# Weight groups 5 to 10 loaded in four pieces of 32 partitions, each later piece held back to a later attention unit

## The chip, the cores and the metric

One Trainium2 chip, one of its cores. The program is launched once for the whole layer. The metric is the device time of one execution in microseconds (us), lower is better; where several runs are given, their median counts. The core has five engines with instruction queues of their own, which run in order: TensorE (PE, with its weight loads shown apart as PEld), VectorE (DVE), ScalarE (ACT), GpSimd (POOL) and SyncE (SP). SP's queue (SPq) issues nearly all of the DMAs here, the DMA transposes among them; POOL issues the loads of the weights.

## The reference

One layer over 1024 tokens of width 1024, in float32: an RMS norm, one input projection to 3328 columns, two groups of heads that read the same projected input, a SiLU gate on each, one output projection, the residual and a last RMS norm.

```python
h = _rmsnorm(x, norm_gain[l])
proj = h @ w_in[l]
q_a, k_a, v_a, g_a, q_b, k_b, v_b, g_b = jnp.split(proj, split_at, axis=-1)
q_a = _rmsnorm(q_a.reshape(b, s, A_HEADS, HEAD_DIM), q_norm_a[l])
k_a = _rmsnorm(k_a.reshape(b, s, A_KV_HEADS, HEAD_DIM), k_norm_a[l])
q_a = q_a * cos + _rotate_half_axial(q_a) * sin
k_a = k_a * cos + _rotate_half_axial(k_a) * sin
o_a = _gqa_blocked(q_a, k_a, v_a) * jax.nn.silu(g_a)
o_b = _neighbourhood_attn(q_b, k_b, v_b, na_rpb[l]) * jax.nn.silu(g_b)
x = x + jnp.concatenate([o_a, o_b], axis=-1) @ w_out[l]
return _rmsnorm(x, final_norm_gain)
```

Group A is full attention with 8 query heads and 2 key/value heads; group B is attention over a window of a 16 by 64 token grid. (Reshapes and the per-head details of group B are cut.)

## The kernel before

The columns of the input projection are cut into 13 groups of 256 (0 is k and v of group A, 1 and 2 its queries, 3 and 4 the queries of B, 5 and 6 its keys, 7 and 8 its values, 9 to 12 the gates), those of the output projection into four more (13 to 16). Every product is done with float32 numbers split into a high and a low half of 16 bits, so each group of weights goes through four steps:

- `load_w(g)`: 1 MB from memory into the tile `raw{g}`, 128 partitions by 8 KB. There are two such buffers (`wraw`, bufs=2), so the load of group g + 2 waits until group g has been split.
- `prep_a(g)`, L280: ACT squares `raw{g}` and sums it up.
- `prep_b(g)`, L292 to L294: PE, DVE and POOL turn the sum into a scale; the last step is a power on POOL (L294).
- `prep_c(g)` and `prep_d(g)`, L299 and L306: ACT writes the high half, DVE the low half, into `whl{g}`. From then on PE may use the group.

`Flow` strings the work together in slots. `step` runs, in this order, what is due at "pre", a first piece of work, what is due at "mid", a second one, what is due at "post", then some pieces of projection from a queue (`fill`), and a last one. `at(n, pos, fn)` puts `fn` n slots later at that position. When a group has been split, `sums_now` puts `load_w(g + 2)` two slots later at "pre".

Stage A is 64 units (head half, block of 128 queries, head), one for each slot. Unit i has `a_qk` as its first piece: four matmuls give the scores `s` (L591, L593), DVE finds the maximum (L600) and writes it into the small tile `nm`, ACT takes the exponential (L602) and the high half of it (L603). One slot later `a_lo` takes the low half on DVE (L608) and issues from SP a DMA transpose of both halves, 128 x 2048 x 2 bytes (L613, `ar<-ar` or `pt<-ar`). Four slots after `a_qk` (SKEW_A = 4) `a_pv` multiplies the transposed probabilities with the values (L622 to L624). Between these, PE works on projection groups 3 to 8 in small pieces of 6 matmuls (L368, tiles `pj`, `wt`, `kb`). Their results are brought into shape by ACT and DVE, and for the queries of B by one more transpose each (L504), for the keys of B by four plain DMAs (L537, tile `khh`).

PE runs in the order in which the program is written. Outside the opening, the order on ACT, DVE, POOL and SP is settled by a scheduler when the program is built. Weight groups 5 to 10 are loaded in stage A or right ahead of it; POOL has little else to do there, but at the load of group 5 it is still busy with the rotary step of group A's queries (`norm_rope`: L416, L424, L428).

A load can be gated: a one-column copy into the tile that is to be loaded (L157), from a tile that must exist first, makes the DMA behind it wait. Groups 2 and 3 use that.

Of the kernel before, what the change touches and what calls it, by code (L numbers as in the profile page):

```python
# [43 lines left out]
class Flow:  # L44
# [8 lines left out]
    def at(self, delay, pos, fn, *a):  # L53
        self.due.setdefault((self.slot + delay, pos), []).append((fn, a))
# [35 lines left out]
def kernel(ctx: ExitStack, tc: tile.TileContext, x: bass.AP, w: bass.AP, wo: bass.AP,  # L90
# [3 lines left out]
    act, dve, pool, pe, sp = nc.scalar, nc.vector, nc.gpsimd, nc.tensor, nc.sync  # L94
# [10 lines left out]
    at = fl.at  # L105
# [12 lines left out]
    def carve(store, off, shape, dt):  # L118

        n = 4 if dt == F32 else 2  # L120
        t = store[:, off // 4:off // 4 + int(np.prod(shape)) * n // 4]
        t = t if n == 4 else t.bitcast(dt)
        if len(shape) == 1:
            return t
        names = "abcdef"[:len(shape)]
        return t.rearrange(f"p ({' '.join(names)}) -> p {' '.join(names)}", **dict(zip(names, shape)))
# [21 lines left out]
    def tn(name, n=1, tag="t"):  # L148
        return tiny.tile([P, n], F32, tag=tag, name=name)


    raw, wp, late, x2 = {}, {}, {}, {}

    def load_w(g):
        raw[g] = wraw.tile([P, KC, GC], F32, tag="raw", name=f"raw{g}")
        if g in gate:
            pool.tensor_copy(raw[g][:, 0, :1], xr[gate[g]][:, 1:])  # L157
        pool.dma_start(raw[g], w[g] if g < 13 else wo[g - 13])

    xts, gate = [], {}  # L160
    ones = area(0, [P], F32)[:1]
# [35 lines left out]
    def col(i, n=1):  # L197
        return sm[:, i:i + n]
# [141 lines left out]
    def sums_now():  # L340

        while pend:
            g = pend.pop(0)
            prep_b(g)
            at(1, "pre", prep_c, g)
            at(1, "post", prep_d, g)
            if g + 2 < 17:
                at(2, "pre", load_w, g + 2)
# [238 lines left out]
    def a_qk(i, hh, u, h):  # L587
        s = ps_s.tile([P, 1024], F32, tag="s", name=f"s{hh}_{u}_{h}")
        q = qTa[hh][:, u, h]
        for c in range(2):  # L590
            pe.matmul(s[:, c * 512:(c + 1) * 512], q, kTa[:, 4 * c:4 * c + 4, hh], start=True, stop=False)  # L591
        for c in range(2):
            pe.matmul(s[:, c * 512:(c + 1) * 512], q, klo1[:, 4 * c:4 * c + 4] if hh else kTa[:, 4 * c:4 * c + 4, 2],  # L593
                      start=False, stop=True)
        if h == 0:
            sums[hh, u] = tn(f"sum{hh}_{u}", 4, "sum")
        nm = tn(f"nm{hh}_{u}_{h}")
        o = 4096 * (i % RING)
        hl, p32 = carve(ar, o, [2, 1024], F16), carve(ar, o + 2048, [1024], F32)
        dve.tensor_tensor_reduce(out=hl[:, 1].bitcast(BF16), in0=s, in1=col(SHA).to_broadcast([P, 1024]), scale=col(NSA),  # L600
                                 scalar=3e38, op0=OP.add, op1=OP.min, accum_out=nm)
        act.activation(p32, s, AF.Exp, bias=nm, scale=col(SCA), accum_out=sums[hh, u][:, h:h + 1])  # L602
        at(0, "post", lambda: act.activation(hl[:, 0], p32, AF.Copy))  # L603
        hls[hh, u, h] = (hl, p32)
# [266 lines left out]
    x_rs(7)  # L871
    x_y(7)
    load_w(2)
    gate[3] = 5
    x_lo(7, dve)
    load_w(3)

    for p in range(11):
# [33 lines left out]
    n_head = sum(n for n, _ in FILL_A)  # L912
    mid = (6 * 32 - sum(n * r for n, r in FILL_A) - FILL_A_END * SKEW_A) / (64 - n_head) + 0.02
    run_units(ua, SKEW_A, a_qk, a_lo, a_pv, rates(FILL_A + [(64 - n_head, mid)], FILL_A_END))
    fl.fill(1000)

# [127 lines left out]
```

## Time and profile before

| | us |
|---|---|
| median of 3 runs | 599.39 |
| the 3 runs | 599.29, 599.39, 605.95 |
| profiled execution, its time | 600.28 |
| profiled execution, its span (first to last instruction) | 598.5 |
| PE busy | 530.8 (89% of the span) |
| DVE busy | 440.9 (74%) |
| ACT busy | 391.0 (65%) |
| POOL busy | 121.8 (20%) |
| mean granted TensorE clock | 0.974 |

Times in the profile are counted from the first instruction of the span. A row of the timeline reads: start, duration, engine, line, operation, the tile written and the tiles read, and in square brackets the idle time of the engine just before it and what ended it. In the chain of waits each row is a start, a duration and what the time was spent on; a row "DMA ar<-ar" there is the time from a transpose's issue to its landing. Stage A runs from about 105 us to about 350 us.

### The profile page before, as it was taken

The numbers are of one execution on the slowest core, as the hardware profiler recorded it, in microseconds if no ns is written. First come the engines' busy times: TensorE is split into PE (matmuls) and PEld (weight loads), VectorE is DVE, ScalarE is ACT, GpSimd is POOL, SyncE is SP. The second block draws the span as 40 slices with busy tenths as digits, with TensorE's granted clock in tenths as the row PEclk, the third lists the DMA queues.
The fourth block names the chain that finished last, engine by engine and source line by source line (L and its number), as shares of the span: only waits on it lengthen the run. The fifth ranks groups of instructions, "written<-read, shape, count | busy, mean of one in ns | idle before, by whom it ended". The sixth has DMA issues, their size and how long they took to land.

```text
span 598.5 us, 13870 instructions
## 1 busy us (share of the span) xinstructions
PE 530.8 (89%) x5541; PEld 404.4 (68%) x5541; DVE 440.9 (74%) x986; ACT 391.0 (65%) x647; POOL 121.8 (20%) x150
## 2 busy tenths in 40 slices
PE   2587989979979989998989979999999789889894
PEld 1366878758856545556768857887877567668684
DVE  4689676987978968975988947585878767778332
ACT  5553445777768858875868826677779986774210
POOL 2395788510100000000100000010111221122100
PEclk9979989989999989999899999999999899999898
DMA  8989533799999999999899983467576996699422
GB/s 233 225 162 243 112 108 68 143 187 215 195 192 188 206 209 181 221 191 208 179 188 213 230 214 79 90 133 96 128 116 123 180 200 146 138 146 190 92 61 70
DMA packets 245972, 97.26 MB, mean 162 GB/s; under 512 B 236562, under 2 KB 237202, under 8 KB 243987
## 3 DMA queue, kind: packets, MB, share of 16 engines
q1 hardware_dynamic: 242306, 75.66, 70.8%
q0 software_dynamic: 3312, 19.92, 11.7%
q8 instruction: 43, 0.70, 0.5%
q10 hardware_dynamic: 288, 0.79, 0.5%
q14 instruction: 23, 0.18, 0.1%
HBM read 31.33 MB, written 4.19 MB: 59 GB/s over the span
## 4 chain that ended last, share of the span: by engine, by line
PE 48%; DMA 18%; DVE 14%; issue 8%; ACT 5%; POOL 4%; SPq 1%; DVEq 0%; POOLq 0%; ACTq 0%
PE pj L368 15%; DMA ar<-ar 10%; PE wt L368 8%; PE kb L368 5%; PE po L368 4%; PE s L591 3%; PE s L593 3%; PE pv L622 2%; PE pv L624 2%; PE pv L623 2%; DVE whl L306 2%; DMA ar<-mhl 2%; POOL nt L416 1%; PE sb L675 1%; DMA x2b<-in_x_dram 1%
## 5 line engine op out<-in xcount | busy, mean ns | idle before, releaser
L368 PEld LDWEIGHTS <-hT 128*128 128x128 f16 x2112 | 205.8, 100 | 68.9 <-DMA hT<-xhl 14.7
L368 PE MATMUL pj<-whl,hT 128*128 128x256 f16 x1584 | 187.6, 274 | 3.9 <-DMA hT<-xhl 2.5
L602 ACT ACTIVATE ar<-s,nm,sm 128x1024 f32<-128x1024 f32 x64 | 76.9, 1202 | 43.6 <-DVE nm L600 35.8
L600 DVE CUSTOM_DVE_ANT_0 ar<-s,sm 128x1024 bf16<-128x1024 f32 x64 | 81.9, 1279 | 18.9 <-PE s L593 18.6
L368 PE MATMUL wt<-whl,hT 128*128 128x256 f16 x528 | 70.9, 294 | 13.8 <-ACT whl L299 7.1
L608 DVE TENSOR_TENSOR ar<-ar 128x1024 f16<-128x1024 f32 x64 | 77.9, 1218 | 5.4 <-ACT ar L603 5.4
L603 ACT ACTIVATE ar<-ar 128x1024 f16<-128x1024 f32 x64 | 67.5, 1056 | 6.5 <-DVE ar L608 5.3
L368 PE MATMUL po<-whl,mA 128*128 128x256 f16 x384 | 65.8, 277 | 0.0
L685 ACT ACTIVATE rq<-ar,mx,sm 128x384 f32<-128x384 f32 (+1 forms) x64 | 43.0, 672 | 30.8 <-DVE mx L684 30.6
L294 POOL TENSOR_TENSOR sm<-wss,mh 128x1 f32<-128x1 f32 x17 | 12.7, 749 | 240.4 <-DVE wss L293 160.6
L368 PEld LDWEIGHTS <-mA 128*128 128x128 f16 x512 | 48.8, 100 | 12.5 <-issue 5.3
L368 PE MATMUL po<-whl,ar 128*128 128x256 f16 x192 | 53.1, 277 | 0.0
L622 PE MATMUL pv<-va,ar 128*128 128x64 f16 x384 | 39.9, 195 | 12.0 <-DMA ar<-ar 12.0
L306 DVE SCALAR_TENSOR_TENSOR whl<-raw,sm,whl 128x1024 f16<-128x1024 f32 (+1 forms) x33 | 44.7, 1371 | 2.3 <-ACT whl L299 2.3
L622 PEld LDWEIGHTS <-ar 128*128 128x128 f16 x384 | 35.1, 99 | 16.6 <-DMA ar<-ar 14.3
L686 ACT ACTIVATE ar<-ar,mx,sm 128x384 f16<-128x384 f32 (+1 forms) x64 | 42.8, 673 | 1.0
L299 ACT ACTIVATE whl<-raw,sm 128x1024 f16<-128x1024 f32 x34 | 37.0, 1136 | 5.9 <-POOL sm L294 5.8
L624 PE MATMUL pv<-va,ar 128*128 128x64 f16 x384 | 39.9, 195 | 0.0
L623 PE MATMUL pv<-va,ar 128*128 128x64 f16 x384 | 39.8, 195 | 0.0
L591 PE MATMUL s<-kTa,rq 128*128 128x512 f16 x128 | 39.4, 391 | 0.3 <-ACT ar L602 0.3
L682 DVE CUSTOM_DVE_ANT_0 ar<-sb,bias 128x384 f32<-128x384 f32 x48 | 26.6, 554 | 17.2 <-PE sb L675 14.3
L691 DVE TENSOR_TENSOR ar<-rq,ar 128x384 f16<-128x384 f32 (+1 forms) x64 | 34.1, 533 | 4.4 <-ACT ar L686 4.4
(183 smaller groups left out, 1012.2 us busy)
## 6 DMA issues: line engine op xcount, KB each, us to landing
raw<-in_w_dram POOLq DMA_DIRECT2D x11, 1024.0 KB, 6.3
raw<-in_wo_dram POOLq DMA_DIRECT2D x4, 1024.0 KB, 6.1
ar<-in_x_dram SPq DMA_DIRECT2D x7, 512.0 KB, 6.4
khh<-ar SPq DMA_DIRECT2D x16, 128.0 KB, 4.1
x2b<-in_x_dram POOLq DMA_DIRECT2D x4, 512.0 KB, 6.4
x<-in_x_dram POOLq DMA_DIRECT2D x4, 512.0 KB, 6.3
out_dram<-x2b SPq DMA_DIRECT2D x8, 256.0 KB, 3.3
ar<-ar SPq DMA_TRANSPOSE x112, 4.5
```

What stands on the lines that cost most here:

```text
L306: dve.scalar_tensor_tensor(wp[g][1][:, s], raw[g][:, s], col(S_ + g), wp[g][0][:, s], op0=OP.mult, op1=OP.subtract)
L368: pe.matmul(*o[0], **o[1])
L591: pe.matmul(s[:, c * 512:(c + 1) * 512], q, kTa[:, 4 * c:4 * c + 4, hh], start=True, stop=False)
L600: dve.tensor_tensor_reduce(out=hl[:, 1].bitcast(BF16), in0=s, in1=col(SHA).to_broadcast([P, 1024]), scale=col(NSA), scalar=3e38, op0=OP.ad ...
L602: act.activation(p32, s, AF.Exp, bias=nm, scale=col(SCA), accum_out=sums[hh, u][:, h:h + 1])
L603: at(0, "post", lambda: act.activation(hl[:, 0], p32, AF.Copy))
L608: dve.tensor_tensor(hl[:, 1], p32, hl[:, 0], op=OP.subtract)
L622: pe.matmul(o, pt[:, kt], va[:, kt, hh, 0], start=kt == 0, stop=False)
L623: pe.matmul(o, pt[:, kt], va[:, kt, hh, 1], start=False, stop=False)
L624: pe.matmul(o, pt[:, 8 + kt], va[:, kt, hh, 0], start=False, stop=kt == 7)
L685: act.activation(p32, t, AF.Exp, bias=mx, scale=col(SCB + hh), accum_out=sums["b", u][:, h:h + 1])
L686: act.activation(hl[:, 0], t, AF.Exp, bias=mx, scale=col(SCB + hh))
```

## The change

Only `load_w` and one line of `a_qk` differ. For groups 5 to 10 the one load of 1 MB becomes four of 256 KB, each of 32 partitions by 8 KB. Piece 0 is issued where the whole load was. Pieces 1, 2 and 3 are put one, two and three slots later, at "post"; each has ahead of it on POOL a one-column copy of the newest `nm` into its own 32 partitions, so that it can't start before DVE has found the maximum of the unit of that slot. `late["nm"]` is where `a_qk` leaves that tile.

```diff
         if g in gate:
             pool.tensor_copy(raw[g][:, 0, :1], xr[gate[g]][:, 1:])
-        pool.dma_start(raw[g], w[g] if g < 13 else wo[g - 13])
+        src = w[g] if g < 13 else wo[g - 13]
+        if not 5 <= g < 11:
+            pool.dma_start(raw[g], src)
+            return
+
+        def piece(j):
+            r = slice(32 * j, 32 * j + 32)
+            if j:
+                pool.tensor_copy(raw[g][r, 0, :1], late["nm"][r])
+            pool.dma_start(raw[g][r], src[r])
+        piece(0)
+        for j in range(1, 4):
+            at(j, "post", piece, j)
...
-        nm = tn(f"nm{hh}_{u}_{h}")
+        nm = late["nm"] = tn(f"nm{hh}_{u}_{h}")
```

PE, DVE, ACT and SP have the same instructions in the same order as before. POOL has 36 rows more: 18 copies and 18 DMA issues. All lines behind the edit stand 12 lines lower in the changed kernel (L294 is L306 there, L416 is L428, L424 is L436, L428 is L440).

POOL at the load of group 5 (`raw_1066`), where stage A begins, before; `nt` and `tabs` belong to the rotary step, `sm` holds the scales of the weights:

```order
L158 DMA raw_1066<-in_w_dram 128x2048
L416 TENSOR_TENSOR nt_2_993<-nt_2_993,mh 128x8
L424 TENSOR_TENSOR ar<-ar,tabs 128x8x32 x2
L428 TENSOR_TENSOR ar<-ar 128x512
L416 TENSOR_TENSOR nt_3_1061<-nt_3_1061,mh 128x8
L424 TENSOR_TENSOR ar<-ar,tabs 128x8x32 x2
L428 TENSOR_TENSOR ar<-ar 128x512
L294 TENSOR_TENSOR sm<-wss_1198,mh 128x1
```

The same place of the changed kernel; `nm_0_1` is the maximum of unit 1, and so on:

```order
L167 DMA raw_1066<-in_w_dram 32x2048
L428 TENSOR_TENSOR nt_2_993<-nt_2_993,mh 128x8
L436 TENSOR_TENSOR ar<-ar,tabs 128x8x32 x2
L440 TENSOR_TENSOR ar<-ar 128x512
L428 TENSOR_TENSOR nt_3_1061<-nt_3_1061,mh 128x8
L166 COPY raw_1066<-nm_0_1_1122 32x1
L167 DMA raw_1066<-in_w_dram 32x2048
L436 TENSOR_TENSOR ar<-ar,tabs 128x8x32 x2
L166 COPY raw_1066<-nm_0_2_1163 32x1
L167 DMA raw_1066<-in_w_dram 32x2048
L440 TENSOR_TENSOR ar<-ar 128x512
L166 COPY raw_1066<-nm_0_3_1209 32x1
```

Pieces 1 and 2 of group 5 now stand ahead of the last two steps of the rotary work; the third stands behind it.

POOL at the load of group 7 (`raw_1848`), in the middle of stage A, before:

```order
L294 TENSOR_TENSOR sm<-wss_1616,mh 128x1
L158 DMA raw_1848<-in_w_dram 128x2048
L294 TENSOR_TENSOR sm<-wss_2278,mh 128x1
```

And of the changed kernel, where the tile is `raw_1860`; `nm_3_3` is unit 15, `nm_4_0` unit 16, `nm_4_1` unit 17:

```order
L306 TENSOR_TENSOR sm<-wss_1628,mh 128x1
L167 DMA raw_1860<-in_w_dram 32x2048
L166 COPY raw_1860<-nm_3_3_1927 32x1
L167 DMA raw_1860<-in_w_dram 32x2048
L166 COPY raw_1860<-nm_4_0_1977 32x1
L167 DMA raw_1860<-in_w_dram 32x2048
L166 COPY raw_1860<-nm_4_1_2039 32x1
L167 DMA raw_1860<-in_w_dram 32x2048
L306 TENSOR_TENSOR sm<-wss_2296,mh 128x1
```

The three later pieces follow their units with nothing else between; the loads of groups 6, 8, 9 and 10 look the same.

## The prediction

> **What bounds the kernel now.** I read the page first, for the busy shares, then PE's timeline in stage A for where PE stands idle, then the chain of waits for what ended each of these gaps, then POOL's timeline for the weight loads. The page's first lines:
>
> ```profile
> PE 530.8 (89%) x5541; PEld 404.4 (68%) x5541; DVE 440.9 (74%) x986; ACT 391.0 (65%) x647; POOL 121.8 (20%) x150
> ```
>
> PE is the bound, so what counts are its gaps. Two rows of the chain of waits, the score matmuls of two successive units with no gap between, give the pace of stage A while nothing disturbs it: 158.30 - 154.77 = 3.53 us for a unit.
>
> ```profile
> 154.77 0.43 PE s L591 x2
> 158.30 0.43 PE s L591 x2
> ```
>
> PE's timeline shows where it stops in stage A for a transpose that has not landed; the number in brackets is the gap:
>
> ```profile
> 169.88 0.20 PE L622 MATMUL pv<-va,ar 128*128 128x64 f16 x1 [2.35 <-DMA ar<-ar]
> 177.64 0.20 PE L622 MATMUL pv<-va,ar 128*128 128x64 f16 x1 [1.19 <-DMA ar<-ar]
> 216.34 0.23 PE L622 MATMUL pv<-va,ar 128*128 128x64 f16 x1 [2.51 <-DMA ar<-ar]
> 258.77 0.20 PE L622 MATMUL pv<-va,ar 128*128 128x64 f16 x1 [1.24 <-DMA ar<-ar]
> 302.55 0.20 PE L622 MATMUL pv<-va,ar 128*128 128x64 f16 x1 [2.69 <-DMA ar<-ar]
> 347.09 0.20 PE L622 MATMUL pv<-va,ar 128*128 128x64 f16 x1 [2.03 <-DMA ar<-ar]
> ```
>
> The chain of waits shows the transposes that ended them, issue and time to landing:
>
> ```profile
> 161.13 8.70 DMA ar<-ar
> 170.78 6.82 DMA ar<-ar
> ...
> 207.61 8.69 DMA ar<-ar
> ...
> 251.50 7.22 DMA ar<-ar
> ...
> 295.96 6.55 DMA ar<-ar
> ```
>
> All 64 transposes of stage A, their time in SP's queue (shortest, median, longest, in ns) and their time to landing in us:
>
> ```profile
> L613 SPq DMA_TRANSPOSE ar<-ar x48: 1474/2687/6295, 111.0 to 345.0; - x48
> ...
> DMA to landing us min/median/max: 4.3/5.0/8.7
> ```
>
> So a transpose lands after 4.3 us when nothing is beside it, and these five need 6.55 to 8.70. What is beside them stands in POOL's timeline, the loads of groups 5 to 10:
>
> ```profile
> 101.54 0.64 POOL L158 DMA_DIRECT2D raw<-in_w_dram  x1
> 130.02 0.64 POOL L158 DMA_DIRECT2D raw<-in_w_dram  x1 [4.90 <-DVE whl L306]
> 160.17 0.57 POOL L158 DMA_DIRECT2D raw<-in_w_dram  x1 [4.46 <-DVE sm L355]
> 204.58 0.57 POOL L158 DMA_DIRECT2D raw<-in_w_dram  x1 [5.11 <-DVE whl L306]
> 248.13 0.57 POOL L158 DMA_DIRECT2D raw<-in_w_dram  x1 [5.51 <-DVE whl L306]
> 293.85 0.57 POOL L158 DMA_DIRECT2D raw<-in_w_dram  x1 [4.26 <-DVE whl L306]
> ```
>
> Four of the loads (160.17, 204.58, 248.13, 293.85) are each followed within 3.4 us by the issue of a slow transpose, and PE stops for it. The loads at 101.54 and 130.02 have no such gap behind them. The gap at 347.09 follows the load of group 11, which the change leaves whole. What the change can touch is 2.35 + 1.19 + 2.51 + 1.24 + 2.69 = 9.98 us of gaps. One of them costs more than its length, as windows of 2 us show (the third number from the end is the granted clock):
>
> ```profile
> 214.00:216.00 2.00, 0.00 (x0) 0.00 (x0) 1.55 (x3) 1.52 (x3) 0.00 (x0) 1.00 1.60 102
> 216.00:218.00 2.00, 1.66 (x25) 1.41 (x26) 0.00 (x0) 0.83 (x1) 0.00 (x0) 0.53 1.26 271
> 218.00:220.00 2.00, 2.00 (x7) 0.78 (x6) 0.45 (x1) 0.00 (x0) 0.00 (x0) 0.62 1.13 205
> ```
>
> Behind the gap of 2.51 us PE ran at 0.53 and 0.62 of its clock: 2 x 0.47 + 2 x 0.38 = 1.70 us lost. In all 11.7 us are in reach, 1.95% of the time.
>
> **What a piece costs a transpose.** A whole load adds 8.70 - 4.3 = 4.4 us to the transpose beside it. Lower bound of a piece: nothing, where it finds a pause of the queue; by bytes a quarter, 1.1 us. The nearest row for transfers on fewer partitions is the four plain DMAs of 128 KB on 64 partitions each:
>
> ```profile
> 204.61 2.88 SPq L537 DMA_DIRECT2D khh<-ar  x4
> ```
>
> 2.88 / 4 x 2 = 1.44 us for 256 KB. The upper bound is 4.4 us, a delay that doesn't shrink with the size. I take p = 1.3 us, between 1.1 and 1.44, since those rows are nearest in size.
>
> **What four pieces add up to.** Each piece falls on another unit. A unit lasts 3.53 us and its transpose holds SP's queue for 2.69 (median above), so 0.84 us are free in each unit, and four pieces leave the transposes late by 4 x (p - 0.84). At the load of group 7 the queue also carries the transposes of B's queries, about one for every 2.7 units (8 pieces of projection at about 3 a unit):
>
> ```profile
> 177.35 1.25 SPq L504 DMA_TRANSPOSE qTb<-ar  x1
> ```
>
> They take 1.25 / 2.7 = 0.47 us a unit, and 0.37 us stay free. How much lateness PE bears: 4.4 us late gave gaps of 2.35 and 2.51, so about 2.0 us are covered. With p = 1.3:
>
> - group 7: 4 x 0.93 - 2.0 = 1.7 us of gap where 2.35 + 1.19 = 3.54 stood: gains 1.8.
> - group 8: 4 x 0.46 = 1.8, covered: gains 2.51 and the 1.70 of clock, 4.2.
> - group 9: the same, gains 1.24.
> - group 10: the transpose is issued at 295.96, late for reasons of its own, and PE wanted it at 302.55 - 2.69 = 299.86. With 4.3 + 1.3 it lands at 301.56, so 1.7 us stay: gains 1.0.
>
> Together 8.2 us; with p = 1.1 it is 9.3, with 1.44 it is 6.8. Groups 5 and 6 have no gap to lose; their pieces fall on units 1 to 3 and 7 to 9, and I count nothing.
>
> **POOL and the new waits.** In front of POOL's work at the load of group 5 now stand copies and issues. The rows of before, with the price of a copy (min, median, max in ns) and of an issue:
>
> ```profile
> L157 POOL COPY raw<-xs x2: 173/614/1056, 42.5 to 43.5; 128x1 f32<-128x1 f32 x2
> ...
> L158 POOL DMA_DIRECT2D raw<-in_w_dram x11: 548/572/786, 43.9 to 370.4; - x11
> ```
>
> ```profile
> 112.91 1.41 POOL L424 TENSOR_TENSOR ar<-ar,tabs 128x256 f32<-128x256 f32 x2 [0.87 <-ACT ar L496]
> 115.01 2.12 POOL L428 TENSOR_TENSOR ar<-ar 128x512 f32<-128x512 f32 x1 [0.69 <-DVE ar L427]
> ```
>
> A copy and an issue are 0.61 + 0.57 = 1.18 us, ahead of each of these two; POOL idles 0.87 and 0.69 there, so they end 0.31 + 0.49 = 0.8 us later. Behind L428 wait ACT's L442 and DVE's next step, at a place where PE waits for DVE, so I count 0.8 in full. With the shortest copy it is 0.1, with the longest 1.7. Elsewhere the next thing in POOL's queue is a power (L294), and POOL idles ahead of it for longer than the gate lasts, as behind the load of group 6:
>
> ```profile
> 154.23 1.48 POOL L294 TENSOR_TENSOR sm<-wss,mh 128x1 f32<-128x1 f32 x1 [23.57 <-DVE wss L293]
> ```
>
> The gate itself hides: pieces 1 to 3 of group 7 wait for
>
> ```profile
> 165.32 0.08 DVE L600 DVE_READ_ACCUMULATOR2_ANT nm<- 128x1 f32 x1
> 167.99 0.08 DVE L600 DVE_READ_ACCUMULATOR2_ANT nm<- 128x1 f32 x1
> 172.86 0.08 DVE L600 DVE_READ_ACCUMULATOR2_ANT nm<- 128x1 f32 x1
> ```
>
> so the last starts 12.7 us after 160.17. The reader with least room is ACT's square of group 5, 39.5 us after its load began, and its last piece is issued behind the maximum of unit 3:
>
> ```profile
> 117.91 0.08 DVE L600 DVE_READ_ACCUMULATOR2_ANT nm<- 128x1 f32 x1
> ...
> 141.04 1.92 ACT L280 ACTIVATE whl<-raw 128x2048 bf16<-128x2048 f32 x1
> ```
>
> That is 23 us ahead. Lateness of the weights costs nothing; without that cover each load would stall ACT, and the exponentials behind it, by those 12.7 us.
>
> **The sum.** -8.2 + 0.8 = -7.4 us: 600.28 - 7.4 = 592.9 against the profiled execution. Its time lies 0.9 above the median of the runs shown (599.39), so 592.0 for a median.
>
> **The rivals.**
>
> - *All of it goes.* If a piece finds room in every pause, the 11.7 us go whole: 587.7. For it: the gaps are few and each follows one load. Against it: group 10's transpose is issued late in any case. 0.15.
> - *The lateness is only spread.* A piece lies on a quarter of the partitions; if it moves at a lower rate for that, p nears 1.9, and the lateness at the end of four pieces is what one load made at once: group 7 has 4 x 1.53 - 2.0 = 4.1, the others 4 x 1.06 - 2.0 = 2.2 each, 10.8 us of gaps in all and 1.7 of clock, 12.5 against 11.7. That is 600, give or take 3. For it: the khh row, slower per byte than the load; against it: that row reaches only 1.44. 0.24. [...]
> - *Each piece stalls like a load.* If much of the 4.4 us is the price of starting a load beside a transpose, 24 pieces pay it where six loads did. In general the gaps are (4p - 3.5) + 3 x (4p - 5.36) = 16p - 19.6. Halfway, p = 2.75, that is 24.4 us, and with gaps this long I count the clock's 1.70 at all four: 31.2 against 11.7, so 619; at 4.4 it would be 645. It is slower from p = 1.9 on, by over 2% from p = 2.3 on. For it: the slow transposes were all issued 1.0 to 3.4 us behind the issue of a load, near its beginning. Against it: the one at 251.50 lost 2.9 us, the one at 161.13 lost 4.4, so the size of the overlap counts. 0.12.
> - *POOL's delay at the start grows.* The rotary step ends 2 to 4 us later than counted, and stage A begins later: 594 to 596. 0.05.
>
> **How the numbers follow.** The forecast gets 0.44, with a range of its own of 588 to 596. The whole range is 587 to 603: it takes in the forecast, the spread lateness, POOL's delay and most of the first rival, and leaves out the slower one. Two per cent (12 us), about what a measurement of this kernel can tell from no change, is just above what is in reach: faster by more gets 0.12, from the first rival and the lower end of the forecast; slower by more 0.11, nearly all of the third; 0.77 lie within.
>
> **What would show it.** In the changed kernel the transposes behind the loads should land in 5 to 6 us where they took 7 to 8.7; the gaps at L622's counterpart (12 lines lower) behind groups 8 and 9 should be gone, behind groups 7 and 10 be 1 to 2 us, and the one behind group 11 stay; no clock below 0.9 should stand behind group 8. ACT's squares should wait for no DMA. I am wrong if the longest landings stay near 8 us, if several transposes in a row land in more than 6 us, or if new gaps stand at groups 5 and 6.

## The result and the profile after

| | before | after |
|---|---|---|
| median of 4 runs each, us | 601.22 | 608.42 |
| lowest and highest, us | 599.29, 605.95 | 606.53, 611.81 |
| profiled execution, its time, us | 600.28 | 609.27 |
| its span, us | 598.5 | 607.5 |
| mean granted TensorE clock | 0.974 | 0.969 |

The ratio is 1.0118, with a 95% interval of 1.0072 to 1.0165: the change makes the kernel about 7 us slower. Here and below, ratios and intervals leave out executions more than 1.5% above the fastest of their kernel, while medians and ranges take in all. The forecast was 592.0 with a range of 587 to 603. The page of the changed kernel shows the same work on PE, DVE and ACT as before, and 23 us more on POOL:

```profile
PE 533.5 (88%) x5541; PEld 403.6 (66%) x5541; DVE 441.1 (73%) x986; ACT 390.9 (64%) x647; POOL 144.9 (24%) x186
```

What PE waited for a transpose of the probabilities (us in all, times, longest), from the waits of before:

```profile
PE pv L622 <- DMA ar<-ar: 12.0, 6, 2.7
PE pv L622 <- DMA pt<-ar: 0.3, 1, 0.3
```

and of the changed kernel:

```profile
PE pv L634 <- DMA ar<-ar: 15.0, 12, 2.3
PE pv L634 <- DMA pt<-ar: 3.4, 2, 1.7
```

12.3 us became 18.4, in twice as many waits. PE's timeline of the changed kernel shows where (the gap is in brackets):

```profile
139.78 0.20 PE L634 MATMUL pv<-va,pt 128*128 128x64 f16 x1 [1.72 <-DMA pt<-ar]
145.08 0.20 PE L634 MATMUL pv<-va,ar 128*128 128x64 f16 x1 [1.60 <-DMA ar<-ar]
154.24 0.20 PE L634 MATMUL pv<-va,ar 128*128 128x64 f16 x1 [1.27 <-DMA ar<-ar]
...
174.58 0.20 PE L634 MATMUL pv<-va,ar 128*128 128x64 f16 x1 [0.28 <-DMA ar<-ar]
178.46 0.20 PE L634 MATMUL pv<-va,ar 128*128 128x64 f16 x1 [0.18 <-DMA ar<-ar]
183.45 0.20 PE L634 MATMUL pv<-va,ar 128*128 128x64 f16 x1 [1.94 <-DMA ar<-ar]
...
222.36 0.20 PE L634 MATMUL pv<-va,ar 128*128 128x64 f16 x1 [1.06 <-DMA ar<-ar]
...
264.52 0.20 PE L634 MATMUL pv<-va,ar 128*128 128x64 f16 x1 [2.32 <-DMA ar<-ar]
...
306.43 0.20 PE L634 MATMUL pv<-va,ar 128*128 128x64 f16 x1 [1.31 <-DMA ar<-ar]
311.17 0.20 PE L634 MATMUL pv<-va,ar 128*128 128x64 f16 x1 [1.04 <-DMA ar<-ar]
...
330.19 0.20 PE L634 MATMUL pv<-va,ar 128*128 128x64 f16 x1 [1.62 <-DMA ar<-ar]
```

The first three gaps, 4.59 us, stand where before had none: behind the loads of groups 5 and 6. The next three belong to group 7, then one each to groups 8 and 9, the next two to group 10; a gap of 0.39 us at 315.26 is not shown. The one of 1.62 stands 20 us behind the last piece of group 10 (issued at 310.04), where before had none. Two more, 2.00 and 1.69 us, follow the load of group 11, which stays whole; before had 2.03 and 0.27 there.

A ledger of the 9.0 us between the two spans can be made from DVE's timeline, where each unit of stage A starts its maximum (L600 before, L612 after). Two of its rows before, units 7 and 11:

```profile
135.18 1.28 DVE L600 CUSTOM_DVE_ANT_0 ar<-s,sm 128x1024 bf16<-128x1024 f32 x1
...
149.72 1.27 DVE L600 CUSTOM_DVE_ANT_0 ar<-s,sm 128x1024 bf16<-128x1024 f32 x1
```

and after:

```profile
136.83 1.28 DVE L612 CUSTOM_DVE_ANT_0 ar<-s,sm 128x1024 bf16<-128x1024 f32 x1
...
156.98 1.27 DVE L612 CUSTOM_DVE_ANT_0 ar<-s,sm 128x1024 bf16<-128x1024 f32 x1
```

These four units took 14.54 us before and 20.15 after. All stretches in the same way:

| stretch | before, us | after, us | difference | the prediction's term |
|---|---|---|---|---|
| start to unit 7 | 135.18 | 136.83 | +1.65 | +0.8 (POOL) |
| units 7 to 11 (groups 5, 6) | 14.54 | 20.15 | +5.61 | 0 |
| units 11 to 20 (group 7) | 33.71 | 33.83 | +0.12 | -1.8 |
| units 20 to 29 | 29.70 | 29.87 | +0.17 | |
| units 29 to 30 (group 8) | 6.42 | 3.45 | -2.97 | -4.2 |
| units 30 to 41 | 36.96 | 37.06 | +0.10 | |
| units 41 to 43 (group 9) | 7.54 | 10.30 | +2.76 | -1.24 |
| units 43 to 47 | 19.90 | 17.72 | -2.18 | |
| units 47 to 63 (group 10) | 55.25 | 57.67 | +2.42 | -1.0 |
| unit 63 to the end | 259.30 | 260.62 | +1.32 | |
| sum | 598.5 | 607.5 | +9.0 | -7.4 |

The 2.18 us between units 43 and 47 are no work of the change: DVE waits there for the bias table, 5.16 us before (first row, L648) and 2.98 after (second row, L660), because the changed kernel comes to it 7.4 us later while the table lands only 5.3 us later:

```profile
281.55 1.82 DVE L648 SCALAR_TENSOR_TENSOR ar<-ar,sm 128x1536 f32<-128x1536 f32 x1 [5.16 <-DMA ar<-in_rpb_dram]
```

```profile
286.81 1.82 DVE L660 SCALAR_TENSOR_TENSOR ar<-ar,sm 128x1536 f32<-128x1536 f32 x1 [2.98 <-DMA ar<-in_rpb_dram]
```

Of the changes at groups 7 to 9 the granted clock makes up about half. Windows of 2 us of the changed kernel (third number from the end), behind the gaps of group 7, group 8 and group 9:

```profile
184.00:186.00 2.00, 2.00 (x16) 1.04 (x14) 0.00 (x0) 1.84 (x3) 0.00 (x0) 0.50 1.23 282
186.00:188.00 2.00, 2.00 (x14) 1.48 (x13) 1.62 (x3) 0.29 (x1) 0.00 (x0) 0.69 1.29 262
...
222.00:224.00 2.00, 1.64 (x29) 1.17 (x30) 1.10 (x1) 1.97 (x3) 1.61 (x2) 1.00 1.27 327
...
266.00:268.00 2.00, 2.00 (x6) 0.76 (x5) 1.33 (x3) 0.94 (x2) 0.00 (x0) 0.50 1.08 184
268.00:270.00 2.00, 2.00 (x16) 0.93 (x15) 1.10 (x1) 1.97 (x3) 0.00 (x0) 0.71 1.28 270
```

- Group 7: gaps 3.54 before, 0.28 + 0.18 + 1.94 = 2.40 after, so 1.14 gained; but the clock fell here to 0.50 and 0.69, 2 x 0.50 + 2 x 0.31 = 1.62 us. Net +0.5, measured +0.1.
- Group 8: the gap went from 2.51 to 1.06 and the clock stayed at 1.00, which saves 1.45 + 1.70 = 3.15; measured 2.97.
- Group 9: the gap grew from 1.24 to 2.32, and the clock fell to 0.50 and 0.71, 1.58 us: +2.7, measured +2.76.

How the loss at groups 5 and 6 begins shows in POOL's timeline, where the later pieces of group 5 are issued:

```profile
111.91 0.70 POOL L166 COPY raw<-nm 32x1 f32<-32x1 f32 x1
112.91 0.61 POOL L167 DMA_DIRECT2D raw<-in_w_dram  x1 [0.29 <-POOL raw L166]
...
116.86 0.56 POOL L167 DMA_DIRECT2D raw<-in_w_dram  x1 [0.29 <-POOL raw L166]
117.49 1.26 POOL L440 TENSOR_TENSOR ar<-ar 128x512 f32<-128x512 f32 x1
...
120.17 0.53 POOL L167 DMA_DIRECT2D raw<-in_w_dram  x1 [0.29 <-POOL raw L166]
```

L440 is the last rotary step; it ends at 118.75, where before had 117.13. SP's timeline shows the transposes that stand in its queue beside these loads, first of the changed kernel, then of before:

```profile
118.30 5.79 SPq L516 DMA_TRANSPOSE qTb<-ar  x1
124.20 5.37 SPq L625 DMA_TRANSPOSE ar<-ar  x1
```

```profile
117.71 1.94 SPq L504 DMA_TRANSPOSE qTb<-ar  x1
119.75 3.03 SPq L613 DMA_TRANSPOSE ar<-ar  x1
```

Two transposes hold the queue for 5.79 + 5.37 = 11.2 us instead of 5.0. Before, the load of group 5 was over by then: it was issued at 101.54, and no load of L158 took longer than 8.2 us to land. Its window of 104 to 108 us, ahead of these transposes, shows it passing (the last number is GB/s):

```profile
104.00:108.00 4.00, 4.00 (x35) 3.21 (x34) 3.10 (x6) 2.22 (x4) 2.28 (x3) 1.00 1.10 250
```

In the changed kernel three quarters of it are put off until the transposes are under way, and in the window where they meet the DMA engines are nearly as busy as before and move a third as much, 61 GB/s against 183 (after, then before):

```profile
120.00:124.00 4.00, 0.16 (x2) 0.00 (x0) 3.81 (x10) 3.94 (x8) 0.53 (x1) 0.80 0.94 61
```

```profile
120.00:124.00 4.00, 0.79 (x24) 0.79 (x25) 3.65 (x10) 3.31 (x6) 0.35 (x1) 0.99 1.12 183
```

### The profile page after: what moved, and what is told of

It is laid out like the page before. It is cut to its first block, busy times and chain, and to the rows that moved or that the text cites. A ratio compares the mean times of both kernels' runs of the same rounds, so it can differ in the third digit from the quotient of the medians.

```text
span 607.5 us, 13937 instructions
## 1 busy us (share of the span) xinstructions
PE 533.5 (88%) x5541; PEld 403.6 (66%) x5541; DVE 441.1 (73%) x986; ACT 390.9 (64%) x647; POOL 144.9 (24%) x186
## 4 chain that ended last, share of the span: by engine, by line
PE 39%; DMA 18%; issue 15%; DVE 14%; POOL 8%; ACT 4%; SPq 1%; DVEq 0%; POOLq 0%; ACTq 0%
PE pj L380 12%; DMA ar<-ar 10%; PE wt L380 5%; PE kb L380 5%; PE po L380 4%; PE s L605 2%; PE s L603 2%; POOL nt L428 2%; DVE ar L612 2%; DVE whl L318 2%; DMA ar<-mhl 2%; POOL ar L440 2%; POOL ar L436 2%; PE pv L634 1%; DVE ar L620 1%
## 5 line engine op out<-in xcount | busy, mean ns | idle before, releaser
L380 PE MATMUL pj<-whl,hT 128*128 128x256 f16 x1584 | 189.6, 276 | 4.0 <-DVE va L473 1.6
L612 DVE CUSTOM_DVE_ANT_0 ar<-s,sm 128x1024 bf16<-128x1024 f32 x64 | 81.8, 1278 | 22.2 <-PE s L605 21.7
L380 PE MATMUL wt<-whl,hT 128*128 128x256 f16 x528 | 68.2, 286 | 14.5 <-DVE xs L257 6.2
L306 POOL TENSOR_TENSOR sm<-wss,mh 128x1 f32<-128x1 f32 x17 | 12.9, 760 | 180.5 <-DVE wss L305 138.9
```

Source lines behind the costliest of these rows:

```text
L380: pe.matmul(*o[0], **o[1])
```

## The experiments

The first reading of the two traces gave this theory: most of the loss is group 5, whose load was harmless where it stood and collides with the first transposes of stage A where it is held; pieces of 32 partitions make the collision worse. Rivals: POOL's copies and issues in front of the rotary step; the splitting itself, wherever it is done; the hold, wherever it is put. Each edit is shown against the changed kernel. All ratios are against the kernel before.

**Without group 5.** Groups 6 to 10 as in the change, group 5 whole as before.

```diff
-        if not 5 <= g < 11:
+        if not 6 <= g < 11:
```

> Groups 6 to 10 in held pieces of 32 partitions, group 5 whole again. The change put unit 11 of stage A 7.3 us later than before (1.7 us of it by unit 6, where POOL's rotary step was late) and the end of the stage 7.7 us. Start theory (the loss is made by group 5's pieces, at the start of stage A, through POOL and through the transposes there): unit 11 at most 1 us later than before, the run 596 to 601 us. Shape theory (pieces of 32 partitions are what slows transposes, wherever they are): unit 11 still 3 to 5 us later, 604 to 608. Spread theory (holding a load back over four units makes it meet more transposes): the same, 604 to 608.

Measured: 603.13 against 601.18, ratio 1.0013 (0.9965 to 1.0060). Unit 11 starts 0.4 us later than before, not 7.3. Group 8 gains 1.8 us by the same ledger, and group 9 loses 3.0, as in the change. So groups 6 to 10 alone cancel out, and the loss of the change goes with group 5. The ten runs are wide, though: seven lie between 597.98 and 606.70 us, three between 608.11 and 616.56.

**Group 5 alone.**

```diff
-        if not 5 <= g < 11:
+        if g != 5:
```

> Only group 5 in held pieces of 32 partitions, 6 to 10 whole. Start theory: unit 11 late by 6 us or more and the run 605 to 609 us. Shape and spread theory: group 5 has one share in six, unit 11 late by 2 to 4 us (POOL's 1.7 and what its own pieces do), the run 601 to 604.

Measured: 608.09 (ten runs, 602.88 to 613.14), ratio 1.0095 (1.0051 to 1.0140). With the first run's 0.13% this makes 1.08%, against 1.18% for the whole change. The trace has most of the loss in one step: unit 7 starts 1.7 us later than before, unit 8 7.5. SP's timeline of this kernel:

```profile
119.23 6.02 SPq L516 DMA_TRANSPOSE qTb<-ar  x1
125.35 5.65 SPq L625 DMA_TRANSPOSE ar<-ar  x1
...
132.46 5.86 SPq L625 DMA_TRANSPOSE pt<-ar  x1
```

and PE's gap that follows:

```profile
142.40 0.24 PE L634 MATMUL pv<-va,pt 128*128 128x64 f16 x1 [4.38 <-DMA pt<-ar]
```

Three transposes hold the queue for about 6 us each. The third runs beside the whole load of group 6, issued at 132.36; before, one beside that load took 5.20 and made no gap, since the queue was not late by then. PE, four units behind, meets their lateness 17 us after the last piece was issued at 121.09.

**POOL's part alone.** The loads whole as before; only the three copies of group 5 stay on POOL, into a tile that nobody reads.

```diff
         def piece(j):
-            r = slice(32 * j, 32 * j + 32)
-            if j:
-                pool.tensor_copy(raw[g][r, 0, :1], late["nm"][r])
-            pool.dma_start(raw[g][r], src[r])
-        piece(0)
+            pool.tensor_copy(idle[32 * j:32 * j + 32], late["nm"][32 * j:32 * j + 32])
+        pool.dma_start(raw[g], src)
```

(and `if g != 5` for the line above, and the tile `idle`)

> Loads as before; only the three copies of group 5 stand in POOL's queue, into a small tile of their own, no DMA split. If POOL's delay of the rotary step was the 1.7 us by which unit 6 was late: unit 6 late by 1 us or more, ratio 1.002 to 1.004. If that lateness came from the transposes: unit 6 late by less than 0.7 us, ratio 0.998 to 1.002.

Measured: 600.83 against 601.72, ratio 0.9979 (0.9944 to 1.0013). The copies alone cost nothing that can be measured. But this kernel has no delay of the rotary step to test: the last step ends at 117.90, with unit 0 starting 0.75 us later than before, so on time, where in the change it ends at 118.75. The three DMA issues were not tried alone. Two other things speak against POOL's delay as the cause: the first slow transpose of the change begins at 118.30, before the late step has ended, and the kernel with the pieces at units 4 to 6 (below) loses time with its last rotary step at 116.66, not late at all.

**The place alone.** Group 5 whole, but held as a whole until the maximum of unit 2; the other groups as before. (The scheduler lets two transposes, of `qTb` and `rq`, change places here.)

```diff
+        def held():
+            pool.tensor_copy(raw[g][:, 0, :1], late["nm"])
+            pool.dma_start(raw[g], src)
+        at(2, "post", held)
```

> Only group 5 differs from before: one whole load of 1 MB, all partitions, held back until the maximum of unit 2 (about 114 us instead of 101.5), so that it runs beside the first transposes of stage A. In SP's queue the transposes of the queries of A and B change places twice. Placement theory (the loss at group 5 comes from moving its load out of the quiet time ahead of stage A, whatever its shape): units 8 to 11 late by 4 us or more, ratio 1.006 to 1.010. Shape theory (32 neighbouring partitions are needed for it): late by 2 us at most, ratio 0.998 to 1.004.

Measured: 604.14 against 600.80, ratio 1.0038 (1.0014 to 1.0062). Units 8 and 11 start at 138.13 and 152.19, where before has 138.00 and 149.72: 2.5 us are lost, between what the two theories gave. The later place alone costs 0.38%, where the held pieces of 32 partitions cost 0.95%; the two intervals still overlap a little. That the rest comes with the shape of the pieces is what the run with pieces by columns (below) shows.

**Another place.** Group 5 alone, with pieces 1 to 3 at units 4, 5 and 6.

```diff
-            at(j, "post", piece, j)
+            at(j + 3, "post", piece, j)
```

(and `if g != 5`)

> Only group 5 differs from before: piece 0 of 32 partitions at its old place, pieces 1 to 3 held to units 4, 5 and 6 instead of 1, 2 and 3; the copies then stand behind the rotary step in POOL's queue. If any piece of 32 partitions inside stage A stalls the transposes: one transpose of 9 us or more again and a step of 4 to 6 us in the units 8 to 14, ratio 1.006 to 1.010. If it took the one meeting of piece 2 with the transpose of B's queries near 119 us: no such step, ratio 0.998 to 1.003.

Measured: a median of 618.60 over ten runs, which lie between 599.78 and 623.95. The ratio, 1.0058 (1.0005 to 1.0110), comes from three of the ten. The profiled execution, at 619.05, shows what can happen. First a transpose in SP's timeline, and the whole load of group 6 in POOL's:

```profile
134.42 22.35 SPq L625 DMA_TRANSPOSE ar<-ar  x1
```

```profile
130.04 0.56 POOL L160 DMA_DIRECT2D raw<-in_w_dram  x1 [0.61 <-DVE whl L318]
```

PE's gap comes next, and from the chain of waits the transpose that ended it (issue and time to landing); it stands right ahead of the other in SP's queue:

```profile
155.43 0.24 PE L634 MATMUL pv<-va,ar 128*128 128x64 f16 x1 [15.04 <-DMA ar<-ar]
```

```profile
129.62 25.76 DMA ar<-ar
```

and the windows in between:

```profile
144.00:148.00 4.00, 0.00 (x0) 0.00 (x0) 0.00 (x0) 0.00 (x0) 0.00 (x0) 0.67 0.83 61
148.00:152.00 4.00, 0.00 (x0) 0.00 (x0) 0.00 (x0) 0.00 (x0) 0.00 (x0) 0.50 1.11 57
```

No engine works in these 8 us; the DMA engines' share is 0.83 and 1.11, within the 0.79 to 1.27 that before has in its windows from 112 to 152 us, and they move 61 and 57 GB/s. The jam does not belong to the units beside the rotary step, then. But this place differs in one more thing: pieces 2 and 3 of group 5 are issued at 128.88 and 133.52, on either side of group 6's whole load, and the longest landing of a whole load in this execution,

```profile
DMA to landing us min/median/max: 5.5/6.3/25.6
```

fits that load, 130.04 + 25.6 = 155.6, when PE's gap ends. So whole loads jam too, and whether it takes the pieces' shape or only two loads and the transposes at once was not separated here. The ten times are uneven: against the 600.80 of before one is 1 us shorter, two are 5 to 7 longer and seven 13 to 23. Only one was profiled, so that they all come from such a jam is not shown.

**Pieces by columns.** As the change, but each piece is all 128 partitions of a quarter of the columns.

```diff
-            r = slice(32 * j, 32 * j + 32)
+            c = slice(2 * j, 2 * j + 2)
             if j:
-                pool.tensor_copy(raw[g][r, 0, :1], late["nm"][r])
-            pool.dma_start(raw[g][r], src[r])
+                pool.tensor_copy(raw[g][:, 2 * j, :1], late["nm"])
+            pool.dma_start(raw[g][:, c], src[:, c])
```

> As the change, groups 5 to 10, the same hold, but each piece takes all 128 partitions and a quarter of each one's 8 KB. Shape theory: the long landings (10 us at 116 and 135 us) fall to 5 to 6 us, unit 11 is late by POOL's 1.7 us only, the gaps behind groups 7 and 8 go, the run 594 to 600 us. Start theory: unit 11 late by 5 us or more, 605 to 609. Spread theory: as the change, 605 to 609.

Measured: 600.41 against 601.18, ratio 0.9986 (0.9943 to 1.0030). Unit 11 starts 1.2 us later than before, not 7.3, with group 5 held at the same units; group 9 gains 1.1 where the change loses 2.8. This run and the change differ in the shape of the pieces and, with it, in POOL's copies (the last rotary step ends at 117.37 here), so most of the loss needs the 32 partitions. The gaps behind groups 7 and 8 did not go, as the shape theory had it: 0.33, 1.98 and 1.92 us are left. The time from issue to landing (shortest, median, longest, us) of the pieces in this kernel:

```profile
L167 POOL DMA_DIRECT2D raw<-in_w_dram x24: 536/537/637, 101.5 to 302.8; - x24
...
DMA to landing us min/median/max: 3.3/4.7/6.3
```

and in the changed one:

```profile
L167 POOL DMA_DIRECT2D raw<-in_w_dram x24: 489/492/613, 101.3 to 310.0; - x24
...
DMA to landing us min/median/max: 3.3/5.1/9.8
```

The medians are alike; what differs is the longest. Held pieces of 32 partitions reach 9.8 us in the change, 7.3 without group 5, 10.3 with group 5 alone and 23.5 in the run before this (where a whole load reached 25.6); held pieces by columns never pass 6.4 in the three kernels that have them.

**Columns, without group 5.** The two edits above together.

> Held pieces by columns (all 128 partitions) for groups 6 to 10, group 5 whole: no work more on POOL at the start of stage A, and smoothed loads behind. From the units of the run with held column pieces for 5 to 10 (1.2 us late by unit 6, 1.2 us early at the end of stage A): end of stage A 1.5 to 3 us ahead of before, ratio 0.993 to 0.999. If the gain there was chance: 1.000, give or take 0.004.

Measured: 599.87 against 601.72, ratio 0.9960 (0.9928 to 0.9993): a small gain in the times. The profiled execution, 603.30, is one of the longer ones and does not show it: its stage A ends 3.0 us late, with 3.3 lost between units 58 and 59, well behind group 10's last piece.

**Without the hold, 32 neighbouring partitions.** Groups 6 to 10, the four pieces issued at once where the whole load was.

```diff
-            if j:
-                pool.tensor_copy(raw[g][r, 0, :1], late["nm"][r])
...
-            at(j, "post", piece, j)
+            piece(j)
```

> Groups 6 to 10 in four pieces of 32 partitions, all four issued at once where the whole load was (no copy, no wait), group 5 whole. Shape theory: slower than before by 3 us or more, with gaps longer than the 2.35 to 2.69 us that stood behind the whole loads, 603 to 608 us. Spread theory: as before, 599 to 602. Start theory: as before, 599 to 602, since group 5 is whole.

Measured: 612.13, ratio 1.0186 (1.0130 to 1.0243). Group 7's gap is

```profile
176.62 0.23 PE L632 MATMUL pv<-va,ar 128*128 128x64 f16 x1 [6.18 <-DMA ar<-ar]
```

where the whole load left 2.35. Against the same pieces held (1.0013) this is 1.7%: the hold does help, once the load is split. (The unheld kernel was run four times.)

**Without the hold, other shapes.** The same with partitions j, j + 4, j + 8 and so on in piece j,

```diff
-            r = slice(32 * j, 32 * j + 32)
+            r = slice(j, P, 4)
```

> As the unheld pieces of 32 partitions (groups 6 to 10, four at once, 612 us against 601 before, ratio 1.019), with the same bytes and the same rows of 8 KB, but piece j takes every fourth partition (j, j + 4, ...) instead of 32 neighbours. If it is the neighbourhood of the partitions that jams the transposes: ratio 0.995 to 1.005, no stretch of 5 us and more for a load with packets of 3 us and more. If it is the number of partitions or of transfers: ratio 1.015 to 1.02 again, with gaps of 4 to 6 us behind group 7.

and with pieces by columns (the edits of both kernels shown above).

> Groups 6 to 10 in four pieces of all 128 partitions by a quarter of the columns, all four issued at once, no hold. If it is the number of transfers that costs: ratio 1.01 or more, as with the unheld pieces of 32 partitions. If it is the partitions: ratio 0.997 to 1.004, gaps behind groups 7 to 10 as before (2.4, 2.5, 1.2, 2.7 us).

Measured: 608.39, ratio 1.0093 (1.0056 to 1.0130), and 607.40, ratio 1.0084 (1.0057 to 1.0111). Both lie between what the theories gave. Splitting without holding costs 0.8 to 0.9% in either shape, and neighbouring partitions another 0.9%. So the shape has a price of its own, but about half of the split's price is there without it: group 7's gap is 4.48 and 5.78 us here, not far from 6.18, and the longest landings of a piece are 9.5 and 10.5 us against 10.7.

**Groups 8 and 9 alone, by columns.** The pieces by columns, held, only for the two groups that gained in that form.

```diff
-        if not 5 <= g < 11:
+        if g not in (8, 9):
```

> Held pieces by columns for groups 8 and 9 alone, where the units of all earlier runs with held pieces by columns came earlier (2.0 to 3.2 us at group 8, 1.1 at group 9); the rest as before. If these gains are the gaps of 2.5 and 1.2 us and the 1.7 of clock that the prediction counted: end of stage A 3 to 5 us earlier, ratio 0.991 to 0.996. If later units give it back: 0.997 to 1.001.

Measured: 597.60 (twelve runs, 594.12 to 599.56) against 600.80, ratio 0.9943 (0.9916 to 0.9969). It is faster than both kernels. The gaps behind the two groups in PE's timeline, 2.51 and 1.24 before, are now

```profile
213.31 0.20 PE L634 MATMUL pv<-va,ar 128*128 128x64 f16 x1 [0.76 <-DMA ar<-ar]
260.42 0.20 PE L634 MATMUL pv<-va,pt 128*128 128x64 f16 x1 [0.41 <-DMA pt<-ar]
```

By the ledger group 8 gains 3.2 us and group 9 1.4. That is 4.6 us in this one execution; at the end of stage A 2.9 are left, and the runs give 600.80 - 597.60 = 3.2. This kernel also shows how far a ledger of single executions can be trusted: ahead of group 8 its program is that of before, and yet its units start up to 1.6 us earlier there, and 0.1 later at others.

| kernel | groups | pieces | held | ratio | interval |
|---|---|---|---|---|---|
| the change | 5 to 10 | 32 partitions | yes | 1.0118 | 1.0072 to 1.0165 |
| | 6 to 10 | 32 partitions | yes | 1.0013 | 0.9965 to 1.0060 |
| | 5 | 32 partitions | yes | 1.0095 | 1.0051 to 1.0140 |
| | 5 | 32 partitions, at units 4 to 6 | yes | 1.0058 | 1.0005 to 1.0110 |
| | 5 | whole | yes | 1.0038 | 1.0014 to 1.0062 |
| | 5 to 10 | columns | yes | 0.9986 | 0.9943 to 1.0030 |
| | 6 to 10 | columns | yes | 0.9960 | 0.9928 to 0.9993 |
| | 8 and 9 | columns | yes | 0.9943 | 0.9916 to 0.9969 |
| | 6 to 10 | 32 partitions | no | 1.0186 | 1.0130 to 1.0243 |
| | 6 to 10 | every fourth partition | no | 1.0093 | 1.0056 to 1.0130 |
| | 6 to 10 | columns | no | 1.0084 | 1.0057 to 1.0111 |

## Why the prediction was wrong

**The step that failed** is "Groups 5 and 6 have no gap to lose; their pieces fall on units 1 to 3 and 7 to 9, and I count nothing." It asked what the change could take away at these loads, and not what it could put there. The row was in the prediction: group 5's load is issued at 101.54, ahead of the transposes of stage A. Holding it back does not thin out a collision, it makes one: unit 11 is late by 2.5 us with the load held whole, by 1.2 with pieces by columns and by 7.3 with the change's pieces of 32 partitions. Group 5 alone costs 0.95%, and without group 5 the ratio is 1.0013. The sign of my own list of what would show me wrong, new gaps at groups 5 and 6, is what came, and so did its first, with a longest landing of 10.1 us.

**The cost of a piece** was sized too low. Put back into the prediction's formulas, the gaps that came give p = (2.40 + 2.0) / 4 + 0.37 = 1.5 us at group 7, (1.06 + 2.0) / 4 + 0.84 = 1.6 at group 8 and (2.32 + 2.0) / 4 + 0.84 = 1.9 at group 9, where 1.3 was taken. "By bytes a quarter" does not hold: a whole load lands after 5.4 us at the least and 6.1 in the median (before), a quarter of it after 3.3 and 5.1 (after), so four pieces one after the other are on their way more than twice as long as one load (4 x 3.3 = 13.2 us against 5.4, an estimate from these two). The size was a bound by bytes, and the 1.44 of the khh row was time in SP's queue (the same DMAs land after 4.1 us in the median, before); the landing times would have been the row to take.

**The second rival's form.** 1.5 to 1.9 is close to the price of "the lateness is only spread", which gave 600, and without group 5 the kernel is there (603.13, ratio 1.0013). Its p of 1.9 is the price at which four pieces come to the 4.4 us of one load, 4.4 / 4 + 0.84; that a piece moves at a lower rate because it lies on a quarter of the partitions was the author's assumption, and no run shows the cause. The runs agree in sign, with 1.0186 for neighbours and 1.0093 for every fourth partition, both unheld. But every fourth partition and columns lose 0.8 to 0.9% as well, and the longest landing of all, 25.6 us (6.3 in the median of that kernel), is that of a whole load, which lies on all 128 partitions.

**The clock** was counted where the trace of before showed a drop, at group 8, and there the 1.70 came in full: the group gained 2.97 us of the 4.2 forecast, the rest being mostly the gap of 1.06 that stayed. But two other gaps, of 1.94 and 2.32 us, were followed by 0.50, for 1.62 and 1.58 us, where before the clock had stayed at 1.00 behind gaps of 2.35 and 2.69. That turned group 7's gain to nothing and more than doubled group 9's loss. I had given the clock a term only for the slower rival.

**Group 10** was forecast at -1.0 and came out with the units 47 to 63 at +2.42. Its gap of 2.69 became four, of 1.31, 1.04, 0.39 and 1.62. The last, between units 58 and 59, is the prediction's omission: units that follow well behind the last piece were not in its sum. The step from unit 58 to 59 is longer than before by 0.7 to 3.3 us in all four kernels that hold pieces of group 10 (either shape), and by at most 0.2 in the eight that don't. A load of a table (L658, 768 KB) is issued at 320.31, between the pieces and this gap, but the kernels without such a step load it too; why the transposes are still late there stays open.

**POOL's 0.8 us** was too little for the step itself: the last rotary step ends 118.75 - 117.13 = 1.6 us later. That it comes through in full is not shown. Counted from the start of unit 0, the change loses 1.83 us up to unit 7; the kernel with group 5 alone, whose POOL work there is that of the change, loses 0.93, and the kernel with group 5 whole, whose POOL work there is that of before, 0.93 too. Differences of this size are within the spread between executions (up to 1.6 us in units whose program is the same, in the kernel with columns at groups 8 and 9).

**Right were** that the readers of the weights have room enough (of ACT's squares only one waits for a load at all, 1.6 us for a group of the output projection, which the change leaves whole), and that group 8 gains.

**What stays open:** what jams. Shown are the circumstances: a piece of 32 neighbouring partitions, several pieces at once, or pieces and a whole load at once, in flight beside transposes; DMA engines busy at a third of the bytes of before (61 GB/s against 183); and, in the kernel with pieces at units 4 to 6, times that change from run to run by 24 us. Why the same pieces of group 6 pass at units 7 to 9, when those of group 5 jam at units 1 to 3 or 4 to 6, was not settled. The transposes of B's queries were beside the jams at group 5 and at group 7, but they were not taken away to try. Nor were pieces by columns put at units 4 to 6.

## What to carry to other kernels

Before a transfer is held back, look at what stands where it goes and not only at what it leaves: a load that no one waits for, in a quiet stretch, is best left there (group 5, held, cost 0.38% whole and 0.95% in pieces of 32 partitions), and each load needs its own verdict (here two of six, changed together, were shown to gain, ratio 0.9943). Where transposes had to pass, pieces by columns did better here than pieces of neighbouring partitions (0.9986 against 1.0118 held, 1.0084 against 1.0186 unheld): try them first. Price a piece by its landing time, not by its share of the bytes (5.1 us in the median for 256 KB, 6.1 for 1 MB). And a gap on PE was worth its length plus, behind those of 1.94, 2.32 and 2.51 us, a clock drop of 1.6 to 1.7 us, which the change took from group 8 and put behind groups 7 and 9.

## What the runs showed of the hardware

- **A quarter of the bytes did not land in a quarter of the time.** 1 MB: 5.4 us at the least, 6.1 in the median (before); 256 KB: 3.3 and 5.1 (the change).
- **A DMA transpose and the loads beside it took several times their usual time.** One of a kind that holds SP's queue for 2.6 us in the median and lands after 4.3 at the least held it for 22.35 us, beside a piece of 256 KB that took 23.5 to land and a load of 1 MB that took 25.6 (5.7 and 6.3 in the median). In 8 us of that the DMA engines moved 57 to 61 GB/s at a busy share of 0.83 to 1.11 (one execution, group 5's pieces at units 4 to 6).
- **Spread of one kernel.** With group 5's pieces at units 4 to 6 the same program took 599.78 to 623.95 us; the kernel with columns at groups 8 and 9 kept within 594.12 to 599.56.
- **The length of a gap did not by itself decide on the clock.** Gaps of 1.94 and 2.32 us (183.45 and 264.52, the change) and of 2.51 (216.34, before) were followed by a granted clock of 0.50 to 0.53, one of 2.69 (302.55, before) by 1.00; what else decided was not shown. The windows of the last:

```profile
302.00:304.00 2.00, 1.45 (x28) 1.10 (x29) 0.90 (x2) 1.29 (x2) 0.00 (x0) 1.00 1.13 253
304.00:306.00 2.00, 2.00 (x20) 1.69 (x19) 1.67 (x4) 1.02 (x2) 0.00 (x0) 1.00 0.94 177
```
